# FFN phases two to four of a two-layer macaron trunk: a second pair of hidden chunks as seven block products, and the late pair one chunk later

## The chip, the cores and the metric

The kernel runs on one core of one Trainium2 chip. The metric is the device time of one execution in microseconds; the time of a kernel is the median of three runs. Beside it stands one profiled execution, whose trace gives every instruction's start and length on each engine: PE (TensorE matmuls), PEld (its weight loads), DVE (VectorE), ACT (ScalarE), POOL (GpSimd), SP (SyncE, which issues nearly all DMAs).

## The reference

Two layers, each with three residual steps on x of 256 tokens by 1024, all in float32:

```python
def _swiglu(h, w_in, w_out):
    gate, up = jnp.split(h @ w_in, 2, axis=-1)
    return (jax.nn.silu(gate) * up) @ w_out
...
    for l in range(DEPTH):
        h = _swiglu(_rmsnorm(x, g[0]), ffn_w_in[l, 0], ffn_w_out[l, 0])
        x = x + 0.5 * _rmsnorm(h, g[1])
        h = _mixer(_rmsnorm(x, g[2]), ...)
        x = x + _rmsnorm(h, g[3])
        h = _swiglu(_rmsnorm(x, g[4]), ffn_w_in[l, 1], ffn_w_out[l, 1])
        x = x + 0.5 * _rmsnorm(h, g[5])
```

The hidden width of an FFN is 2816, so w_in is 1024 x 5632 and w_out 2816 x 1024. The mixer (attention and an mLSTM) is not touched by the change.

## The kernel before

**Phases.** The six residual steps are phases 0 to 5, run one after the other: FFN (0), mixer (1), FFN (2), FFN (3), mixer (4), FFN (5). "FFN phases two to four" are phases 2, 3 and 5. In the profile they begin at about 292, 473 and 762 us. The tokens are two tiles of 128.

**Float32 on TensorE.** Every operand is split in two parts, a high part in a reduced float32 form and the low rest; a product is three matmuls, high x high, low x high and high x low (mm3, lines 504 to 508). Weights come in pieces of 1 MB, DMA'd by SP into wr (every fourth piece into wx) and cut in two halves; halved (L291) makes wh of each on ACT (L295) and wl on DVE (L296).

**An FFN.** The hidden width is 11 chunks of 256. The steps that a chunk c goes through are named in a list, STEPS (L37):

- I c: load two pieces, and 48 matmuls of 512 columns for both token tiles; ACT and DVE make Silu(gate) x up (ffn_hidden, L637); planes (L645) reorders the words on ACT, SP turns them with a DMA transpose (L647), and ready joins them: hT (L653), then hh on ACT (L669) and hl on DVE (L670).
- L c: load and cut the chunk's output piece. O c: 24 matmuls of 512 columns into four banks bk, 12 for each token tile.
- S: one step of pair_tokens, which makes differences of the token blocks for the pair.
- P c: chunks c and c + 1 together (pair). Their two token tiles by two chunks by two halves of the inner width are 2 x 2 block matrices, computed by seven block products (product, L755) in place of eight; the four weight pieces are added to each other on DVE (pair_blocks, L322), each combination is cut like a weight, and the products are combined on DVE and ACT (L769 to L792) to h for token tile 0 and v for token tile 1, each with both chunks. Both are turned like a chunk's h; pair_ready joins them.
- The last chunk, 10, is not computed tokens by hidden units but turned (in_turned, L730 and L735), so that its result needs no transpose; ffn_turned combines it in su (L688 to L690). Its step I10 ends the list. Behind it the output parts of END, chunks 8, 9 and 10, stand written by hand: token 0 of 8, 9 and 10, then token 1.

**What sets the order.** The lines are recorded in program order, and a scheduler places each engine's instructions by its own priorities, so PE's stream mixes neighbouring steps; parts under high_priority (the pair's combinations, ffn_turned) are placed early. From "ending" to "running" (the output parts of END and the next phase's first matmuls) PE's order is the written one. Each engine runs its own list strictly in order. SP's queue holds weight loads and transposes together. Pools of wl, wh and a lent third one let the cutting run some ten halves ahead of PE. The weights lie in host memory in the order in which the steps load them; _pack takes it from STEPS.

In STEPS the pair is P7, behind O4 and ahead of L6 and O5; chunk 9 follows as I9, and the pair's joining is recorded in I9, behind the cut of its first piece (lines 871 and 872).

Of the kernel before, what the change touches and what calls it, by code (L numbers as in the profile page):

```python
# [33 lines left out]
CH = P  # L34
EPS = 1e-6
BIG = -1.0e30
STEPS = "I2 L1 S0 O0 I3 L2 S1 O1 I4 L3 S2 O2 I5 L4 O3 I6 L5 O4 P7 L6 O5 L7 O6 I9 L8 O7 I10 L9".split()  # L37
END = (8, 9, 10)
AHEAD = 2
AT = (0, 2, 6, 6, 9, 22, 24, 24, 26, 26, 36, 40, 30, 46, 34, 50, 46, 52, 52, 57, 61, 60, 61, 67, 67, 69, 71, 78, 74, 74, 80, 84)  # L40
# [19 lines left out]
def _pack(inp):  # L60


    f32 = np.float32
    x = np.asarray(inp["x"])
    w_in, w_out = np.asarray(inp["ffn_w_in"]), np.asarray(inp["ffn_w_out"])
    m_in, m_out = np.asarray(inp["mix_w_in"]), np.asarray(inp["mix_w_out"])
    g = np.asarray(inp["norm_gains"])
    w = np.empty((L * PIECES_LAYER, P, 2048), f32)

    def ffn(at, l, f):  # L70
        n = w_in[l, f].reshape(2, 4, P, 2, NC_FF, 256).transpose(0, 3, 2, 1, 4, 5)
        a = n.transpose(4, 0, 2, 3, 1, 5).reshape(NC_FF, 2, P, 2048)
        b = w_out[l, f].reshape(NC_FF, 2, P, D).transpose(0, 2, 1, 3).reshape(NC_FF, P, 2048)
        order = [a[0, 0], a[0, 1], a[1, 0], a[1, 1], b[0]]
        for step in STEPS:
            c = int(step[1:])
            if step[0] == "P":
                order += [n[kh, g, :, :, c:c + 2].reshape(P, 2048) for kh, g in ((0, 0), (0, 1), (1, 1), (1, 0))]
            elif step[0] in "IL":
                order += [a[c, 0], a[c, 1]] if step[0] == "I" else [b[c]]  # L80
        for piece in order + [b[END[-1]]]:
            w[at] = piece
            at += 1

    for l in range(L):
        at = l * PIECES_LAYER
        ffn(at, l, 0)
        at += PIECES_FFN
        for n, lo in enumerate(MIX_GROUPS):
            a = m_in[l][:, lo:lo + 512].reshape(2, 4, P, 512).transpose(0, 2, 1, 3)  # L90
            w[at + 2 * n:at + 2 * n + 2] = a.reshape(2, P, 2048)
        at += 2 * len(MIX_GROUPS)
        w[at:at + 4] = m_out[l].reshape(4, 2, P, D).transpose(0, 2, 1, 3).reshape(4, P, 2048)
        ffn(at + 4, l, 1)
    for i in range(2):
        w[i] = w[i].reshape(P, 4, 512).transpose(1, 0, 2).reshape(P, 2048)

    arrays = {
        "x": x.reshape(NT, P, 2, 512).transpose(0, 2, 1, 3),
        "w": w,  # L100
        "gpost": g[:, 1::2].reshape(L * 3, D),
        "lam": np.asarray(inp["da_lambda"]).reshape(L, 256),
    }
    arrays = {k: np.ascontiguousarray(v) for k, v in arrays.items()}
    gpre = g[:, 0::2].reshape(L, 3, KT, P).transpose(3, 0, 1, 2).reshape(P, L * 3 * KT)
    arrays["c0"] = np.concatenate([np.eye(P, dtype=f32), gpre], 1)

    inv = (f32(10000.0) ** (-np.arange(0, 64, 2, dtype=f32) / f32(64))).astype(f32)
    ang = np.arange(S, dtype=f32)[:, None] * inv[None, :]
    cos, sin = np.cos(ang).astype(f32), np.sin(ang).astype(f32)  # L110
    rope = np.stack([np.concatenate([cos, cos], 1), np.concatenate([-sin, sin], 1)])
    s = np.arange(P)[:, None]
    j = np.arange(P)[None, :]
    mask = np.where((s // CH == j // CH) & (s <= j), 0.0, BIG).astype(f32)
    first = (np.arange(S) % CH == 0)
    scan = np.stack([np.where(first, 0.0, 1.0), np.where(first, BIG, 0.0)]).astype(f32)

    def everywhere(v):
        return np.broadcast_to(np.asarray(v).reshape(1, -1), (P, np.asarray(v).size))

    parts = {
        "wg": m_in[:, :, 3072:3080].reshape(L, KT, P, 8).transpose(2, 0, 1, 3),
        "rope": rope.reshape(2, NT, P, 64).transpose(2, 0, 1, 3),
        "convw": np.asarray(inp["ml_conv_w"]).reshape(L, 4, 4, P).transpose(3, 0, 2, 1),
        "convb": np.asarray(inp["ml_conv_b"]).reshape(L, 4, P).transpose(2, 0, 1),
        "gda": np.asarray(inp["da_subln_g"]).T,
        "gml": np.asarray(inp["ml_norm_g"]).T,
        "gateb": everywhere(inp["ml_gate_b"]),
    }
    arrays["c1"] = np.concatenate([parts[n].reshape(P, -1) for n, _ in C1], 1)  # L130
    arrays["mask"] = mask
    arrays["scan"] = np.ascontiguousarray(np.broadcast_to(scan.reshape(1, 512), (100, 512)))
    return arrays


class _Trunk:
# [569 lines left out]
    def ffn(self, pre, gi_post):  # L706
# [3 lines left out]
        def in_piece(t, kh, pin, w):  # L710
            xh, xl = xT[t][kh]
            for k in range(4):
                self.mm3(pin, xh[:, k, :], xl[:, k, :], *self.cols(w, k),
                         start=kh == 0 and k == 0, stop=kh == 1 and k == 3)

        def out_part(c, t, h, wo):
            for hf in range(2):
                for k in range(2):
                    self.mm3(po[t][hf], *h[t][k], *self.cols(wo, 2 * k + hf),
                             start=c == 0 and k == 0, stop=c == NC_FF - 1 and k == 1)  # L720
# [20 lines left out]
        def ready(c, others):  # L741
            if c in sent:
                hT = self.ffn_joined(sent.pop(c), others)
                hs[c] = self.ffn_split([hT[:, t] for t in range(NT)])

        def chunk(c, pins):
            h = self.t2("h", (P, NT, 256))
            i = [self.ffn_hidden(pins[t], r[t], h[:, t]) for t in range(NT)]
            send(c, h)
            ready(c - 1, i[:1])  # L750
# [45 lines left out]
        def pair_ready(others):  # L796
            c, turned = sent.pop("pair")
            hT = [self.ffn_joined(v, others) for v in turned]
            for j in range(2):
                hs[c + j] = self.ffn_split([h[:, j] for h in hT])  # L800

        hs, po, wo, sent = {}, [], {}, {}
        kept = bool(xT)
# [48 lines left out]
            ready(0, [i])  # L852
        both, swap = list(self.both), 0
        tokens = self.pair_tokens(both, kept)
        for at, step in enumerate(STEPS):
            kind, c = step[0], int(step[1:])
            if kind == "P":
                pair(c)
            elif kind == "S":
                sums = next(tokens)  # L860
            elif kind == "L":
                if wo.get(c) is None:
                    wo[c] = self.piece()
            elif kind == "I":
                if c == 3:
                    g = self.load_gpost(gi_post)
                    yield "middle"
                ws = [self.piece()]
                cut = self.cut
                ws.append(self.piece())  # L870
                if "pair" in sent:
                    pair_ready([cut])
                for later in STEPS[at + 1:]:
                    if later[0] != "L":
                        break
                    wo[int(later[1:])] = self.piece()
                if c == END[-1]:
                    ready(c - 1, [self.cut])
                    break
                pins = [self.bank_pin() if swap else self.bank_tr() for _ in range(NT)]  # L880
                swap = 1 - swap
                for kh in range(2):
                    for t in range(NT):
                        in_piece(t, kh, pins[t], ws[kh])
                chunk(c, pins)
            else:
                if not po:
                    po = [[self.bank_bk() for _ in range(2)] for _ in range(NT)]
                for t in range(NT):
                    out_part(c, t, hs[c], wo[c])  # L890
# [574 lines left out]
```

## Time and profile before

| | us |
|---|---|
| median of three runs | 953.43 (953.31 to 953.56) |
| profiled execution | 954.38 |
| its span in the trace | 952.6 |
| granted TensorE clock, mean | 0.999 |
| phases 0, 1, 2, 3, 4, 5 begin at about | 0, 183, 292, 473, 653, 762 |

The span is what the trace covers, from the first instruction to the last; the profiled execution's own time is 1.8 us longer. Busy shares are means over the span. The page's sliced rows, 40 slices of 23.8 us each, show how even the load of the engines is (tenths; 9 is 90% or more):

```profile
DVE  7965885789767865795796578857897687558853
ACT  8966767577756866586587657666778478567662
```

The engine beside TensorE that is busiest is DVE; its 8s and 9s lie where the weight cutting of a phase's opening or of a pair falls.

### The profile page before, as it was taken

To read this page: it belongs to the slowest core of one execution; us is meant where nothing else is said; L and a number is where in the kernel's file an instruction comes from. 1 tells how busy PE (TensorE), PEld (TensorE's weight loads), DVE (VectorE), ACT (ScalarE), POOL (GpSimd) and SP (SyncE) were. 2 spreads that over 40 slices of the span, in tenths; PEclk is the share of its full clock that TensorE was granted. 3 is DMA by queue.
4 is the path that set the end of the run, shared out by engine and by line. 5 is a ranking of instruction groups with operands and counts; after the bars stand their busy time and mean duration, and the time that the engine had idled before them with its cause. 6 is when DMAs were issued, how large, how long until landed. Compare 5 with 4: busy or idle time off the path is not lost.

```text
span 952.6 us, 12113 instructions
## 1 busy us (share of the span) xinstructions
PE 944.1 (99%) x4475; PEld 779.7 (82%) x4475; DVE 705.4 (74%) x1011; ACT 648.9 (68%) x1013; POOL 28.0 (3%) x57
## 2 busy tenths in 40 slices
PE   9999999999999999999999999999999999999997
PEld 6888888888788888888888888888888888888885
DVE  7965885789767865795796578857897687558853
ACT  8966767577756866586587657666778478567662
POOL 2000000000010000000000000000000100000000
PEclk9999999999999999999999999999999999999999
DMA  9985476346362885467558663753554449654731
GB/s 342 343 300 151 150 273 201 133 137 235 109 250 89 313 243 182 155 238 234 181 201 284 184 224 128 277 161 133 180 197 157 153 160 291 233 175 143 284 83 45
DMA packets 69881, 189.33 MB, mean 199 GB/s; under 512 B 45274, under 2 KB 46426, under 8 KB 49086
## 3 DMA queue, kind: packets, MB, share of 16 engines
q1 hardware_dynamic: 69246, 187.95, 58.5%
q8 instruction: 35, 0.57, 0.2%
q10 hardware_dynamic: 576, 0.61, 0.2%
q14 instruction: 24, 0.20, 0.1%
HBM read 177.01 MB, written 1.05 MB: 187 GB/s over the span
## 4 chain that ended last, share of the span: by engine, by line
PE 94%; ACT 2%; DMA 1%; DVE 1%; issue 1%; SPq 0%; POOLq 0%; DVEq 0%; ACTq 0%
PE pin L506 11%; PE pin L508 11%; PE pin L507 11%; PE bk L508 10%; PE bk L506 10%; PE bk L507 10%; PE ptr L506 5%; PE ptr L508 5%; PE ptr L507 5%; PE ptr L755 4%; PE pin L755 3%; PE pin L730 2%; PE ptr L730 1%; PE ptr L532 1%; PE ptr L1087 1%; PE pin L735 1%
## 5 line engine op out<-in xcount | busy, mean ns | idle before, releaser
L296 DVE TENSOR_TENSOR wl<-wr,wh 128x1024 fp32r<-128x1024 f32 x262 | 314.7, 1222 | 96.7 <-ACT wh L295 90.7
L295 ACT ACTIVATE wh<-wr 128x1024 fp32r<-128x1024 f32 x262 | 270.1, 1053 | 67.3 <-PE pin L508 18.7
L506 PE MATMUL pin<-wh,both 128*128 128x512 f32 x496 | 196.5, 397 | 0.1
L508 PE MATMUL pin<-wh,both 128*128 128x512 f32 x496 | 193.4, 390 | 0.0
L507 PE MATMUL pin<-wl,both 128*128 128x512 f32 x496 | 193.3, 390 | 0.0
L507 PE MATMUL bk<-wl,hh 128*128 128x512 f32 x352 | 137.1, 389 | 0.0
L506 PE MATMUL bk<-wh,hh 128*128 128x512 f32 x352 | 136.6, 390 | 0.0
L508 PE MATMUL bk<-wh,hl 128*128 128x512 f32 x352 | 135.2, 390 | 0.1
L506 PEld LDWEIGHTS pin<-wh,both 128*128 128x128 f32 x496 | 93.3, 188 | 19.7 <-issue 0.7
L508 PEld LDWEIGHTS pin<-wh,both 128*128 128x128 f32 x496 | 93.1, 188 | 19.9
L507 PEld LDWEIGHTS pin<-wl,both 128*128 128x128 f32 x496 | 93.3, 188 | 18.0
L296 DVE TENSOR_TENSOR wl<-wx,wh 128x1024 fp32r<-128x1024 f32 x62 | 75.3, 1222 | 30.4 <-ACT wh L295 30.4
L295 ACT ACTIVATE wh<-wx 128x1024 fp32r<-128x1024 f32 x62 | 64.5, 1052 | 22.2 <-PE ptr L508 6.8
L508 PEld LDWEIGHTS bk<-wh,hl 128*128 128x128 f32 x352 | 66.1, 188 | 14.4 <-DVE hl L670 0.5
L507 PEld LDWEIGHTS bk<-wl,hh 128*128 128x128 f32 x352 | 66.1, 188 | 13.5
L506 PEld LDWEIGHTS bk<-wh,hh 128*128 128x128 f32 x352 | 66.1, 188 | 13.3
L507 PE MATMUL ptr<-wl,both 128*128 128x512 f32 x192 | 74.7, 389 | 0.0
L508 PE MATMUL ptr<-wh,both 128*128 128x512 f32 x192 | 74.7, 389 | 0.0
L506 PE MATMUL ptr<-wh,both 128*128 128x512 f32 x192 | 73.4, 389 | 0.0
L653 ACT ACTIVATE hT<-h 128x1024 uint16<-128x1024 uint16 x36 | 49.0, 1360 | 15.3 <-DMA h<-planes 15.2
L645 ACT ACTIVATE planes<-h 128x1024 uint16<-128x1024 uint16 x36 | 37.9, 1052 | 19.4 <-DVE h L637 19.2
L670 DVE TENSOR_TENSOR hl<-hT,hh 128x256 fp32r<-128x256 f32 x80 | 30.3, 420 | 19.3 <-ACT hh L669 19.3
(263 smaller groups left out, 1288.7 us busy)
## 6 DMA issues: line engine op xcount, KB each, us to landing
wr<-in_w_dram SPq DMA_DIRECT2D x131, 1024.0 KB, 5.1
wx<-in_w_dram SPq DMA_DIRECT2D x31, 1024.0 KB, 4.9
gpost<-in_gpost_dram SPq DMA_DIRECT2D x6, 512.0 KB, 6.2
wr<-in_w_dram SPq DMA_DIRECT2D x2, 512.0 KB, 7.2
wr<-in_w_dram SPq DMA_DIRECT2D x3, 256.0 KB, 5.5
x<-in_x_dram SPq DMA_DIRECT2D x3, 256.0 KB, 5.9
h<-planes SPq DMA_TRANSPOSE x36, 4.4
out_dram<-x SPq DMA_DIRECT2D x2, 256.0 KB, 2.1
```

Source lines behind the costliest of these rows:

```text
L295: ia = nc.scalar.activation(hi, raw, AF.Copy)
L296: iv = nc.vector.tensor_tensor(lo, raw, hi.bitcast(F32), op=ALU.subtract)
L506: mm(ps, xh, wh, start=start, stop=False)
L507: mm(ps, xh, wl, start=False, stop=False)
L508: mm(ps, xl, wh, start=False, stop=stop)
L532: nc.tensor.transpose(ptr[:, k, :], x[:, (4 * hf + k) * P:(4 * hf + k + 1) * P], self.ident)
L645: nc.scalar.activation(planes, h.bitcast(U16).rearrange("p (n u) -> p u n", u=2), AF.Copy)
L653: i = self.nc.scalar.activation(hT.rearrange("p a b n -> p (a b n)").bitcast(U16).rearrange("p (n u) -> p u n", u=2), turned.rearrange("p ...
L670: return ia, self.nc.vector.tensor_tensor(hl, h, hh.bitcast(F32), op=ALU.subtract)
L730: self.nc.tensor.matmul(b, self.cols(w[kh], k)[0][:, c], both[kh][:, k].rearrange("p i t -> p (i t)"), start=kh == 0 and k == 0, stop=Fals ...
L735: self.nc.tensor.matmul(b[:, 0:NT * P], self.cols(w[kh], k)[1][:, c], both[kh][:, k, 0:NT].rearrange("p i t -> p (i t)"), start=False, sto ...
L755: self.nc.tensor.matmul(b, st[:, k, :], self.cols(w, k)[mv], start=new and k == n == 0, stop=k == 3 and n == 2, skip_group_check=True)
```

## The change

The list of steps becomes two. ONE is the old list and serves phase 0 alone (the phase that makes its own token blocks, kept False). TWO serves phases 2, 3 and 5: chunks 4 and 5 become a pair P4 directly behind O1 and S2; chunk 7 is a chunk of its own again; the late pair is P8, chunks 8 and 9; chunk 10 follows at once. The pair's joining is not recorded ahead of the next input step's weights if that step is I10, but behind the cut of chunk 9's output piece.

```diff
-STEPS = "I2 L1 S0 O0 I3 L2 S1 O1 I4 L3 S2 O2 I5 L4 O3 I6 L5 O4 P7 L6 O5 L7 O6 I9 L8 O7 I10 L9".split()
+ONE = "I2 L1 S0 O0 I3 L2 S1 O1 I4 L3 S2 O2 I5 L4 O3 I6 L5 O4 P7 L6 O5 L7 O6 I9 L8 O7 I10 L9".split()
+TWO = "I2 L1 S0 O0 I3 L2 S1 O1 S2 P4 L3 O2 L4 O3 I6 L5 O4 I7 L6 O5 P8 L7 O6 L8 O7 I10 L9".split()
 END = (8, 9, 10)
...
-        for step in STEPS:
+        for step in TWO if l or f else ONE:
...
-        for at, step in enumerate(STEPS):
+        steps = TWO if kept else ONE
+        for at, step in enumerate(steps):
...
                 ws = [self.piece()]
                 cut = self.cut
                 ws.append(self.piece())
-                if "pair" in sent:
+                if "pair" in sent and c != END[-1]:
                     pair_ready([cut])
-                for later in STEPS[at + 1:]:
+                for later in steps[at + 1:]:
                     if later[0] != "L":
                         break
                     wo[int(later[1:])] = self.piece()
                 if c == END[-1]:
+                    if "pair" in sent:
+                        pair_ready([self.cut])
                     ready(c - 1, [self.cut])
                     break
```

One line is added near the top, so most of the changed kernel's line numbers are one higher: L756 is the product, L646 planes, L648 the transpose, L654 hT, L670 and L671 hh and hl, L731 and L736 in_turned, L689 the copies to su, L323 the adds. The rows below are the order of an engine's instructions; the digits behind a name tell buffers apart.

On PE in phase 2, before, behind the pair: the last matmuls of the earlier output parts (bk), and then chunk 9's own products into pin.

```order
L508 MATMUL bk_3200<-wh_3926,hl_3856 128x512
L506 MATMUL bk_3200<-wh_3930,hh_3855 128x512
L507 MATMUL bk_3200<-wl_3929,hh_3855 128x512
L508 MATMUL bk_3200<-wh_3930,hl_3856 128x512
L506 MATMUL pin_4041<-wh_3994,both_2824 128x512
L507 MATMUL pin_4041<-wl_3993,both_2824 128x512
```

In the changed kernel, at the same place: the pair's last product (ptr_3952), five matmuls of O7, and chunk 10's turned products.

```order
L756 MATMUL ptr_3952<-wh_3936,both_3192 128x512
L508 MATMUL bk_3200<-wl_4070,hh_4000 128x512
L509 MATMUL bk_3200<-wh_4071,hl_4001 128x512
L507 MATMUL bk_3200<-wh_4075,hh_4000 128x512
L508 MATMUL bk_3200<-wl_4074,hh_4000 128x512
L509 MATMUL bk_3200<-wh_4075,hl_4001 128x512
L731 MATMUL pin_4191<-both_2824,wh_4139 128x512 x2
```

Further on, the turned products end and O8's token 0 begins, whose operand hh_4170 is the pair's.

```order
L736 MATMUL ptr_4194<-both_2833,wl_4148 128x256 x2
L736 MATMUL ptr_4194<-both_2833,wl_4152 128x256 x2
L507 MATMUL bk_3197<-wh_4105,hh_4170 128x512
L508 MATMUL bk_3197<-wl_4104,hh_4170 128x512
L509 MATMUL bk_3197<-wh_4105,hl_4171 128x512
```

Chunk 9's 48 matmuls are gone from between the pair and the first use of its words. In phases 3 and 5, 20 matmuls of O7 stand where phase 2 has five.

On ACT in phase 2, before, behind the pair: the pair's Silu, the planes of h and v, and the joinings hT.

```order
L267 ACTIVATE u_3810<-u_3810,rs_589_2968 128x512
L645 ACTIVATE planes_3902<-h_3812 128x1024
L295 ACTIVATE wh_4128<-wr_4125 128x1024
L295 ACTIVATE wh_4132<-wr_4125 128x1024
L645 ACTIVATE planes_3920<-v_3811 128x1024
L653 ACTIVATE hT_4011<-h_3812 128x2x512
L669 ACTIVATE hh_4015<-hT_4011 128x256
```

In the changed kernel the same stretch holds chunk 10's copies to su and its Silu too; hh_4170 is O8's operand for token 0, hh_4178 that of O9.

```order
L689 ACTIVATE su_4265<-pin_4191 128x256
L689 ACTIVATE su_4265<-pin_4192 128x256
L646 ACTIVATE planes_4065<-v_3956 128x1024
L268 ACTIVATE su_4265<-su_4265 128x256
L654 ACTIVATE hT_4166<-h_3956 128x2x512
L670 ACTIVATE hh_4170<-hT_4166 128x256
L689 ACTIVATE su_4278<-ptr_4193 128x256
L689 ACTIVATE su_4278<-ptr_4194 128x256
L654 ACTIVATE hT_4168<-v_3956 128x2x512
L268 ACTIVATE su_4278<-su_4278 128x256
L670 ACTIVATE hh_4172<-hT_4168 128x256
L670 ACTIVATE hh_4178<-hT_4166 128x256
```

Two copies that read in_turned's first banks have moved ahead of the planes of v. In phase 3 of the changed kernel the copies stand behind the joinings:

```order
L646 ACTIVATE planes_5610<-v_5501 128x1024
L654 ACTIVATE hT_5711<-h_5502 128x2x512
L670 ACTIVATE hh_5715<-hT_5711 128x256
L654 ACTIVATE hT_5713<-v_5501 128x2x512
L670 ACTIVATE hh_5717<-hT_5713 128x256
L670 ACTIVATE hh_5723<-hT_5711 128x256
L670 ACTIVATE hh_5725<-hT_5713 128x256
L689 ACTIVATE su_5810<-pin_5736 128x256
```

Both orders are the scheduler's; phase 5 has the one of phase 3.

On DVE in phase 2, before, around the step S2 (the difference aT and its split both): splits of weights and the results of chunks 2 and 3.

```order
L357 TENSOR_TENSOR aT_638_3193<-qk,wt 128x512
L296 TENSOR_TENSOR wl_3239<-wr_3237,wh_3240 128x1024
L670 TENSOR_TENSOR both_3192<-aT_638_3193,both_3192 128x4x128
L296 TENSOR_TENSOR wl_3229<-wr_3227,wh_3230 128x1024
L296 TENSOR_TENSOR wl_3233<-wr_3227,wh_3234 128x1024
L637 SCALAR_TENSOR_TENSOR h_3047<-pin_3046,rs_589_2968,sil_3075 128x256
L296 TENSOR_TENSOR wl_3243<-wr_3237,wh_3244 128x1024
L637 SCALAR_TENSOR_TENSOR h_3171<-ptr_3121,rs_566_2883,sil_3172 128x256
L296 TENSOR_TENSOR wl_3249<-wr_3247,wh_3250 128x1024
L637 SCALAR_TENSOR_TENSOR h_3171<-ptr_3122,rs_589_2968,sil_3175 128x256
```

In the changed kernel:

```order
L358 TENSOR_TENSOR aT_638_3193<-qk,wt 128x512
L297 TENSOR_TENSOR wl_3239<-wr_3237,wh_3240 128x1024
L671 TENSOR_TENSOR both_3192<-aT_638_3193,both_3192 128x4x128
L297 TENSOR_TENSOR wl_3229<-wr_3227,wh_3230 128x1024
L297 TENSOR_TENSOR wl_3233<-wr_3227,wh_3234 128x1024
L638 SCALAR_TENSOR_TENSOR h_3047<-pin_3046,rs_589_2968,sil_3075 128x256
L297 TENSOR_TENSOR wl_3243<-wr_3237,wh_3244 128x1024
L638 SCALAR_TENSOR_TENSOR h_3171<-ptr_3121,rs_566_2883,sil_3172 128x256
L297 TENSOR_TENSOR wl_3249<-wr_3247,wh_3250 128x1024
L323 TENSOR_TENSOR qk<-wx_3360,wr_3362 128x1024
L638 SCALAR_TENSOR_TENSOR h_3171<-ptr_3122,rs_589_2968,sil_3175 128x256
L323 TENSOR_TENSOR wt<-wx_3360,wr_3362 128x1024
```

S2 has kept its place; the first adds of P4's weight blocks (qk and wt are the halves of the sum) follow it where splits of chunk 4's weights stood.

## The prediction

> **What bounds the kernel now.** The page's busy shares come first, then the shares of the chain that ended last.
>
> ```profile
> span 952.6 us, 12113 instructions
> PE 944.1 (99%) x4475; PEld 779.7 (82%) x4475; DVE 705.4 (74%) x1011; ACT 648.9 (68%) x1013; POOL 28.0 (3%) x57
> ...
> PE 94%; ACT 2%; DMA 1%; DVE 1%; issue 1%; SPq 0%; POOLq 0%; DVEq 0%; ACTq 0%
> ```
>
> The end is set by TensorE from the first microsecond to the last: 99% busy, and 94% of the chain. The waits of PE, next, as engine and line, what was waited for, total us, times, longest:
>
> ```profile
> PE bk L495 <- PEq L1455: 0.8, 1, 0.8
> PE ptr L454 <- DMA x<-in_x_dram: 0.7, 1, 0.7
> PE bk L482 <- ACT wh L472: 0.2, 1, 0.2
> ```
>
> All three lie at the start; none lies in a phase that the change touches. So the time is the number of matmuls times their pitch, as long as operands are there. The chain (start, length, what) gives the pitch:
>
> ```profile
> 160.39 1.81 PE pin L730 x8
> 163.11 0.95 PE pin L735 x8
> ...
> 401.96 2.72 PE pin L755 x12
> ...
> 424.63 2.72 PE ptr L755 x12
> ```
>
> Twelve 512-column matmuls take 2.72 us: 0.2267 us each. The 256-column ones of L735 take 0.95 / 8 = 0.119 us.
>
> **What goes.** A pair as block products is 7 x 12 = 84 matmuls where two chunks of their own have 2 x 48 = 96. FFN phases two to four are phases two, three and five of the six, counted from zero; each gets one pair more, P4, and the late pair moves from chunks 7, 8 to 8, 9. That is 12 matmuls fewer in each of three phases: 36 x 0.2267 = **8.16 us** less on PE. The matmul group says that one "lasts" 389 ns, which would make 14.0 us; but that is a latency under pipelining, and the pitch is what adds up.
>
> ```profile
> L755 PE MATMUL ptr<-wh,both 128*128 128x512 f32 x128 | 41.7, 389 | 0.0
> ```
>
> The Trainium skill, page "TensorE: Matmul & The Clock Gate", section "Back-to-back issue gap", gives a sustained spacing of about 131 ns for 512 columns in a stream of weight loads and matmuls, and N/2.4 + 2.5 ns = 216 ns for one alone. The first would make the gain an estimated 4.7 us, the second 7.8; the trace's 0.2267 us stands in such a stream and contradicts the first.
>
> **What is added beside PE.** The groups (total us, mean ns, idle ahead):
>
> ```profile
> L296 DVE TENSOR_TENSOR wl<-wr,wh 128x1024 fp32r<-128x1024 f32 x262 | 314.7, 1222 | 96.7 <-ACT wh L295 90.7 <-PE bk L507 3.6 <-PE bk L508 1.7
> L295 ACT ACTIVATE wh<-wr 128x1024 fp32r<-128x1024 f32 x262 | 270.1, 1053 | 67.3 <-PE pin L508 18.7 <-PE ptr L755 9.8 <-PE bk L508 9.0
> L322 DVE TENSOR_TENSOR wr<-wr,wr 128x1024 f32<-128x1024 f32 x6 | 7.1, 1221 | 4.7 <-DMA wr<-in_w_dram 4.7
> L784 DVE TENSOR_TENSOR h<-ptr,u 128x512 f32<-128x512 f32 x4 | 2.7, 686 | 1.7 <-PE ptr L755 1.7
> L792 DVE SCALAR_TENSOR_TENSOR v<-v,rs,u 128x512 f32<-128x512 f32 x4 | 3.0, 750 | 0.0
> L637 DVE SCALAR_TENSOR_TENSOR h<-pin,rs,sil 128x256 f32<-128x256 f32 x38 | 18.1, 480 | 2.3 <-ACT sil L267 2.3
> L267 ACT ACTIVATE u<-u,rs 128x512 f32<-128x512 f32 x4 | 2.9, 726 | 5.0 <-DVE u L790 5.0
> ```
>
> One more pair brings DVE 8 adds of 1.22 us, 6 more weight splits of 1.22 (14 halves in place of 8), 7 combining operations (five like L784, two like L792: 4.9 us) and takes 4 of L637's away (1.9 us): 9.8 + 7.3 + 4.9 - 1.9 = **20.1 us of DVE a phase**, 60 in all, so 705 becomes about 766 of some 948 (81%). ACT gets 6 casts of 1.05 and a few small ones, about 7 us a phase. DMA bytes and the number of transposes stay.
>
> Spread over a phase this fits; inside a pair it does not. A pair wants (8 + 14) x 1.22 + 4.9 = 31.7 us of DVE against 84 x 0.2267 = 19.0 of PE, 12.7 too much, so it lives on splits made ahead. The windows of the old pair (bounds, length, then busy time of PE, PEld, DVE, ACT, POOL, clock, DMA share, GB/s) show whether that is enough; first phase two's opening up to chunk 3, where P4 will stand, then the stretch ahead of the old pair, then that pair in phases two and three:
>
> ```profile
> 292.00:346.00 54.00, 54.00 (x245) 44.82 (x243) 43.62 (x57) 39.75 (x58) 1.62 (x3) 1.00 0.70 222
> 346.00:402.00 56.00, 56.00 (x248) 46.36 (x248) 35.84 (x39) 33.30 (x40) 0.00 (x0) 1.00 0.59 200
> 402.00:427.40 25.40, 25.40 (x113) 21.02 (x112) 22.55 (x25) 20.67 (x26) 0.00 (x0) 1.00 0.61 212
> ...
> 582.00:609.20 27.20, 27.20 (x122) 22.52 (x121) 24.80 (x26) 19.43 (x23) 0.00 (x0) 1.00 0.61 232
> ```
>
> PE never waited, and DVE was idle 25.40 - 22.55 = 2.85 and 27.20 - 24.80 = 2.40 us within the pair: that is the margin. P8 keeps such a stretch ahead of it. P4 does not: in the opening, 54 us, DVE idles 54.00 - 43.62 = 10.4 us, against 20.2 in the 56 ahead of the old pair. (The third token step, S2, costs nothing new: its three operations stand at the same rows of DVE's order before and after.) The splits made ahead must hold 12.7 us of DVE work for P4, and 10.4 are free. **Bounds for waits inside the pairs: nothing (the old pair's rows) to 12.7 - 10.4 = 2.3 us a phase, 6.9 in all. I take 1 in all**, near the old pair's rows, since those are the same instructions and the matmuls of O2, O3 and O6, O7 stand among the products as cover.
>
> **The join, where I choose a loss.** The old pair's result was wanted only after chunk 9's own 48 matmuls. Phase three's chain shows how long the way is:
>
> ```profile
> 607.73 1.37 PE ptr L755 x6
> ...
> 613.82 0.73 ACT u L267
> 614.54 1.00 ACT planes L645
> ...
> 615.56 7.01 DMA h<-planes
> ...
> 622.65 0.04 ACT hT L653
> ...
> 626.09 0.43 DVE hl L670
> ...
> 626.57 0.50 PE bk L508
> ```
>
> The last product ends at 609.1 (call it E); the first tile's turned words land at 622.57, E + 13.5, and PE waited about 0.5 us at 626.1 for the low part (a wait that the change removes: **-0.5**). ACT's timeline in phase two (start, length; E = 427.35) shows both tiles:
>
> ```profile
> 430.50 1.06 ACT L645 ACTIVATE planes<-h 128x1024 uint16<-128x1024 uint16 x1
> ...
> 433.44 1.06 ACT L645 ACTIVATE planes<-v 128x1024 uint16<-128x1024 uint16 x1
> 434.76 1.38 ACT L653 ACTIVATE hT<-h 128x1024 uint16<-128x1024 uint16 x1 [0.27 <-DMA h<-planes]
> ...
> 442.87 1.37 ACT L653 ACTIVATE hT<-v 128x1024 uint16<-128x1024 uint16 x1 [2.31 <-DMA v<-planes]
> ```
>
> From the end of planes, the first tile took 3.2 us there (434.76 - 431.56), the second 8.4 (442.87 - 434.50); in phase three the first took 7.0. I take the mean of these, 6.2, with 3.2 and 8.4 as ends, and for the second tile 6.6 from the same rows and the queue's landing times:
>
> ```profile
> DMA to landing us min/median/max: 5.3/6.0/7.0
> ```
>
> In the changed order nothing but the rest of O7 and chunk 10's turned products (in_turned) stands between E and O8. in_turned has 32 matmuls of 512 columns and 32 of 256: 7.25 + 3.81 = 11.06 us, with two small transposes of rows 11.3. Each token-0 output part is 12 matmuls, 2.72 us.
>
> Phase two: 5 matmuls of O7 are left, so O8 starts at E + 1.1 + 11.3 = E + 12.4 and O9 at 15.1. ACT ends the first planes near E + 5.1 (four casts are queued ahead; 4.2 in the old row), the words land near 11.3, hT and hh (1.37 and about 0.4) follow: operands at 12.7 to 13.1, a stall of 0.3 to 0.7. But the operand for O9's token 0 is queued on ACT behind the second tile's hT, and the second planes stand behind two copies of chunk 10's first group, which wait for PE at about E + 6.7. They end near 8.6, land near 15.2, and hT, a Silu and two hh put O9's operand at 17.6: 2.1 us after PE, which is at 15.5 by then. **Phase two loses 2.4**, between 0 (landing after 3.2) and 4.2 (after 8.4).
>
> Phase three: 20 of O7 are left (4.5 us), so O8 is at E + 15.8, O9 at 18.5, O10 at 21.2. Both hT stand on ACT ahead of chunk 10's copies. Landing near 14.6 gives O9's operand at 17.2, in time; but the copies, adds and Silu of chunk 10 then start late and end at 21.5 to 22.3: **0.6**, between 0 and 2.5. Phase five has the same order and no loads of a next phase on SP: **0**.
>
> **Sum**, against the profiled execution's own 954.38 us (span 952.6 and 1.8 outside): -8.16 - 0.5 + 2.4 + 0.6 + 1 = -4.7, so 949.7. The three runs' median, 953.43, is 0.95 lower than the profiled one; taken from there, **948.8**.
>
> **Rivals.**
> *Full gain* (no wait anywhere): 953.43 - 8.66 = 944.8. For it: PE idles nowhere but for 0.5 us. Against it: the landing after 8.4 us in phase two.
>
> *The join becomes the bound; slower.* If the two transposes run one behind the other at 7.0 us each, the first tile lands at E + 12.1 and the second at 19.1. In phase two O9's operand is then at 21.5, 6.4 us late; in phases three and five O9's at 21.3 (2.8 late) and chunk 10's chain another 2.5. That is 6.4 + 5.3 + 5.3 = 17.0: 953.43 - 8.66 + 1 + 17.0 = 962.8. It decides once the three joins cost more than 8.66 - 1 + 1.9 = 9.6 us together, a landing at about E + 17 in all three. The rows are against it: in phase two the second tile's planes were cut while the first was landing, and no landing took more than 8.4.
>
> *VectorE becomes the bound in the early pair; no change.* If the 2.3 us of the bound appear in each phase, 6.9 us of waits take most of the gain: 953.43 - 8.66 + 3.0 + 6.9 = 954.7. It decides from 3.7 us in all, where the sum passes 951.5. The deficit of 12.7 us and the busier opening speak for it, the 2.4 us of DVE left idle inside the old pair against it.
>
> *The tensor clock falls.* The windows grant 1.00 throughout and the longest idle stretch is about 0.5 us, so no row shows what a longer one does; the start-up matmuls, which ran from a standstill, are slower than the 389 ns above:
>
> ```profile
> L495 PE MATMUL bk<-const-bfloat16-1.0 128*128 128x512 bf16 x8 | 3.7, 596 | 0.8 <-PEq L1455 0.8
> ```
>
> If phase two's join reaches its upper bound of 4.2 us, and the matmuls behind it run at 389 / 596 = 0.65 of their pace for as much work, that is 1.8 more of a wait and 4.2 / 0.65 - 4.2 = 2.3 of slow matmuls: 948.8 + 4.1 = 952.9. The Trainium skill, page "TensorE: Matmul & The Clock Gate", section "What's actually happening", has the clock halved after an idle window of about 3.4 us; no run here shows it.
>
> *It does not do what it says:* the scheduler undoes it, 953.4. The order has the 36 matmuls gone, so hardly any chance.
>
> **How the numbers follow.** Forecast with partial waits (946.5 to 951.5) 0.50; full gain (943.5 to 946.5) 0.17; VectorE 0.13; join slower 0.13; clock 0.05; nothing 0.02. About 0.2%, 1.9 us, can be told from no change here: below 951.5 is faster (0.67), 951.5 to 955.3 the same (0.20: VectorE, clock, nothing), above it slower (0.13). The range leaves out most of the slower case and the edge of the full gain: 944.5 to 955.5.
>
> **What would show it.** Right: 36 fewer matmuls at the old pitch; PE's gaps only ahead of O9's first matmul (hh or hl of the late pair) in phase two, 2 us, and ahead of O10's in phase three; DVE near 766 us; P4 and P8 with full PE. Wrong: PE waits for wl or wh inside P4; a gap over 3 us ahead of O8 or O9; a granted clock below 1.00 behind a gap; landings beyond E + 17.

## The result, and the profile after

The changed kernel takes **948.88 us** (six runs, 947.47 to 949.17) beside 953.84 us of the kernel before (six runs, 953.31 to 954.52): a ratio of 0.9945, 95% interval 0.9932 to 0.9958. Its profiled execution took 949.07 us, 5.3 less than the one before. The forecast was 948.8.

The page, in the lines that were shown of before:

```profile
span 947.3 us, 12104 instructions
PE 936.2 (99%) x4439; PEld 772.3 (82%) x4439; DVE 757.5 (80%) x1062; ACT 664.5 (70%) x1028; POOL 28.3 (3%) x57
...
PE 97%; DMA 1%; ACT 1%; DVE 0%; issue 0%; SPq 0%; POOLq 0%; DVEq 0%; ACTq 0%
```

36 matmuls fewer (4475 to 4439), and TensorE is still the bound. DVE is busy for 52 us more and is at 80%. (60 were forecast, and the durations of its instructions do add up to 60.6 us more; but neighbours overlap a little, so that two splits in a row take 2.35 us and not 2.44.) The waits of PE are no longer all at the start; beside three such there are now:

```profile
PE bk L507 <- ACT hh L670: 1.7, 1, 1.7
...
PE ptr L507 <- DVE h L785: 0.9, 3, 0.6
```

One wait of an output part (bk) for hh, and three short ones of an input part's bank (ptr) for the pair's combination h (L785). The chain of phase two's end (start, length, what) shows the first; the late pair's last product ends at 445.37:

```profile
442.65 2.72 PE ptr L756 x12
...
452.32 0.39 ACT su L689
452.71 0.94 ACT planes L646
...
453.68 6.67 DMA v<-planes
...
460.37 1.35 ACT hT L654
461.71 0.26 ACT su L268
461.97 0.62 ACT hh L670 x2
...
462.64 0.50 PE bk L507
```

Read from the bottom: O9's first matmul waits for the second hh of tile 0, which stands on ACT behind hT of tile 1 (v), which waits 6.67 us for its transpose. The start of that matmul comes 1.83 us beyond the usual pitch. The second kind, from the same view at the end of P4 in phase two:

```profile
379.21 1.37 PE ptr L756 x6
...
380.61 1.07 ACT wh L296
...
381.70 0.04 DVE wl L297
381.74 1.11 issue
382.85 0.69 DVE h L785
...
383.68 0.47 PE ptr L507
```

The matmul at 383.68 is chunk 6's first. It writes a ptr bank, and the pair's last products lie in the ptr banks until DVE has read them; the read (L785) stands on DVE behind a weight split of 1.2 us. DVE's timeline shows that split:

```profile
381.70 1.23 DVE L297 TENSOR_TENSOR wl<-wr,wh 128x1024 fp32r<-128x1024 f32 x1 [1.72 <-ACT wh L296]
```

DVE stood idle for 1.72 us ahead of it, until ACT had made its wh. The product that L785 reads, the last but one of the seven, had been done since about 377.6, so the read waited for its turn in DVE's queue and not for data. Chunk 6's matmul starts 0.77 us late there, and 0.32 in phases three and five.

The starts of the phases, by the first matmul of each phase's prenorm transposes (L532, now L533) in the timeline, before and after:

| phase | before | after | difference |
|---|---|---|---|
| 2 | 473.37 - 291.19 = 182.18 | 473.72 - 291.34 = 182.38 | +0.20 |
| 3 | 653.51 - 473.37 = 180.14 | 650.91 - 473.72 = 177.19 | -2.95 |
| 5, to the last matmul's start | 945.85 - 761.51 = 184.34 | 940.56 - 758.53 = 182.03 | -2.31 |
| 0, 1 and 4 (unchanged) | 291.19 + 108.00 | 291.34 + 107.62 | -0.23 |

Phase two gained nothing at all; phases three and five gained about the 2.7 us (12 matmuls at their pitch) that each was to gain.

### The profile page after: what moved, and what is told of

It reads as the page before. It is cut to its first block, busy times and chain, and to the rows that moved or that the text cites. A ratio compares the mean times of both kernels' runs of the same rounds, so it can differ in the third digit from the quotient of the medians.

```text
span 947.3 us, 12104 instructions
## 1 busy us (share of the span) xinstructions
PE 936.2 (99%) x4439; PEld 772.3 (82%) x4439; DVE 757.5 (80%) x1062; ACT 664.5 (70%) x1028; POOL 28.3 (3%) x57
## 4 chain that ended last, share of the span: by engine, by line
PE 97%; DMA 1%; ACT 1%; DVE 0%; issue 0%; SPq 0%; POOLq 0%; DVEq 0%; ACTq 0%
PE pin L507 11%; PE pin L509 11%; PE pin L508 11%; PE bk L507 10%; PE bk L509 10%; PE bk L508 10%; PE ptr L756 8%; PE pin L756 6%; PE ptr L507 4%; PE ptr L509 3%; PE ptr L508 3%; PE pin L731 2%; PE ptr L731 1%; PE ptr L533 1%; PE ptr L1091 1%; PE pin L736 1%
## 5 line engine op out<-in xcount | busy, mean ns | idle before, releaser
L507 PE MATMUL pin<-wh,both 128*128 128x512 f32 x448 | 177.0, 398 | 0.0
L509 PE MATMUL pin<-wh,both 128*128 128x512 f32 x448 | 174.7, 390 | 0.0
L508 PE MATMUL pin<-wl,both 128*128 128x512 f32 x448 | 174.6, 390 | 0.0
L509 PE MATMUL bk<-wh,hl 128*128 128x512 f32 x352 | 133.1, 389 | 0.0
L509 PEld LDWEIGHTS pin<-wh,both 128*128 128x128 f32 x448 | 84.1, 188 | 18.0
L507 PEld LDWEIGHTS pin<-wh,both 128*128 128x128 f32 x448 | 84.3, 188 | 17.5 <-issue 0.7
L508 PEld LDWEIGHTS pin<-wl,both 128*128 128x128 f32 x448 | 84.2, 188 | 16.2
L297 DVE TENSOR_TENSOR wl<-wx,wh 128x1024 fp32r<-128x1024 f32 x62 | 75.4, 1222 | 10.4 <-ACT wh L296 10.4
L756 PE MATMUL ptr<-wh,both 128*128 128x512 f32 x224 | 73.3, 389 | 0.0
L507 PE MATMUL ptr<-wh,both 128*128 128x512 f32 x144 | 55.0, 391 | 0.9 <-DVE h L785 0.9
L508 PE MATMUL ptr<-wl,both 128*128 128x512 f32 x144 | 55.7, 389 | 0.0
L509 PE MATMUL ptr<-wh,both 128*128 128x512 f32 x144 | 55.7, 389 | 0.0
L756 PE MATMUL pin<-wh,both 128*128 128x512 f32 x168 | 55.1, 389 | 0.0
L654 ACT ACTIVATE hT<-h 128x1024 uint16<-128x1024 uint16 x33 | 45.0, 1364 | 6.2 <-DMA h<-planes 5.9
```

The costliest lines, as they stand in the source:

```text
L297: iv = nc.vector.tensor_tensor(lo, raw, hi.bitcast(F32), op=ALU.subtract)
L507: mm(ps, xh, wh, start=start, stop=False)
L508: mm(ps, xh, wl, start=False, stop=False)
L509: mm(ps, xl, wh, start=False, stop=stop)
L654: i = self.nc.scalar.activation(hT.rearrange("p a b n -> p (a b n)").bitcast(U16).rearrange("p (n u) -> p u n", u=2), turned.rearrange("p ...
L756: self.nc.tensor.matmul(b, st[:, k, :], self.cols(w, k)[mv], start=new and k == n == 0, stop=k == 3 and n == 2, skip_group_check=True)
```

## The experiments

All times below are medians, with the ratio to the kernel before, which ran beside them: 953.57 us in the first four, 953.92 in the last four. The diffs are against the changed kernel. Phases zero and one are the same program in all but the last kernel, and still phase two begins anywhere from 289.8 to 291.3 us in their traces. So beside the medians this table gives the touched phases alone, from one trace of each kernel but the one with a third pair (starts as in the table above, phase five to its last matmul's start):

| kernel | phase 2 | phase 3 | phase 5 | sum |
|---|---|---|---|---|
| before | 182.18 | 180.14 | 184.34 | 546.66 |
| changed | 182.38 | 177.19 | 182.03 | 541.60 |
| other bank | 181.23 | 176.73 | 181.60 | 539.55 |
| tile 0 first | 180.49 | 177.11 | 182.04 | 539.65 |
| late place alone | 183.89 | 179.67 | 184.36 | 547.92 |
| early pair, old late place | 181.11 | 177.71 | 182.82 | 541.64 |
| both edits | 179.74 | 176.66 | 181.62 | 538.02 |
| joining at its old place | 182.80 | 177.16 | 182.04 | 542.00 |
| both edits, new list everywhere | 179.37 | 179.59 | 181.62 | 540.58 |

**Which bank the chunk behind a pair takes.**

```diff
             if kind == "P":
                 pair(c)
+                swap = 1
```

> The changed kernel, but the chunk behind a pair takes its two banks from pin, not from ptr. Theory (the waits behind P4, start-to-start 0.8, 0.3 and 0.3 us beyond the pitch, are waits for the ptr banks that the pair's last combinations still read on VectorE): they go, about 1.4 us less than the changed kernel, 947.5. Rival (chunk 6 would wait for its weights or VectorE at that place anyway): TensorE waits for wh or wl there instead, 948.9.

947.69 us; ratio 0.9943 (0.9927 to 0.9959). The runs lie far apart (945.69 to 950.82), so the median can't tell 1.4 us; the trace can. (In the three runs at 949 to 951 the granted clock was 0.996 on average, in the three at 945.7 to 946.4 it was 0.998 or 0.999. So the clock seems to have fallen somewhere in the longer ones; no trace of them was kept.) The windows around P4 and chunk 6 in phases two, three and five (bounds, length, busy PE, PEld, DVE, ACT, POOL, clock, DMA share, GB/s):

```profile
350.00:386.00 36.00, 36.00 (x161) 29.80 (x160) 31.63 (x34) 27.34 (x32) 0.00 (x0) 1.00 0.59 214
528.00:566.00 38.00, 38.00 (x169) 31.45 (x169) 35.24 (x38) 29.29 (x33) 0.00 (x0) 1.00 0.61 219
814.00:853.00 39.00, 39.00 (x174) 32.30 (x173) 36.06 (x39) 29.32 (x34) 0.00 (x0) 1.00 0.64 223
```

PE is busy for all of each, so the three waits were for the bank, and nothing took their place. Phase two's wait for hh stays (1.2 and 0.4 us beyond the pitch there). The touched phases are 2.05 us shorter than in the changed kernel.

**Tile 0 first.** For each tile hT and both chunks' hh and hl are made before the next tile is touched.

```diff
-            hT = [self.ffn_joined(v, others) for v in turned]
+            ops = [[self.ffn_operand() for _ in range(2)] for _ in range(NT)]
+            for t in range(NT):
+                hT = self.ffn_joined(turned[t], others)
+                for j in range(2):
+                    self.ffn_hilo(hT[:, j], *ops[t][j])
             for j in range(2):
-                hs[c + j] = self.ffn_split([h[:, j] for h in hT])
+                hs[c + j] = [[tuple(v[:, k] for v in ops[t][j]) for k in range(2)] for t in range(NT)]
```

> The changed kernel, but the joining makes both chunks' operands of token tile 0 before it touches tile 1. Theory (phase two's 1.8 us ahead of O9 come from O9's tile-0 operand being queued on ScalarE behind the joining of tile 1, which waits for its transpose): the wait goes, 947.1, no wait in its place. Rival (the transposes land too late as such): the wait moves to the next output part that needs tile 1 or chunk 10, 948.9.

946.20 us; ratio 0.9925 (0.9913 to 0.9937). ACT's timeline at phase two's join:

```profile
454.94 1.38 ACT L654 ACTIVATE hT<-h 128x1024 uint16<-128x1024 uint16 x1 [2.19 <-DMA h<-planes]
456.35 0.72 ACT L670 ACTIVATE hh<-hT 128x256 fp32r<-128x256 f32 x2
459.44 1.36 ACT L654 ACTIVATE hT<-v 128x1024 uint16<-128x1024 uint16 x1 [1.82 <-DMA v<-planes]
```

Both hh of tile 0 now stand ahead of tile 1's hT. Tile 1 still lands late (459.4, no earlier in the phase than before), and nobody waits: of the 1.8 us, 0.2 ahead of O8 is left. So the order on ACT was the cause, not the landing of tile 1 as such. The touched phases are 1.95 us shorter than in the changed kernel.

**The late place alone.** The old list with P8 in place of P7, and no P4.

```diff
-TWO = "I2 L1 S0 O0 I3 L2 S1 O1 S2 P4 L3 O2 L4 O3 I6 L5 O4 I7 L6 O5 P8 L7 O6 L8 O7 I10 L9".split()
+TWO = "I2 L1 S0 O0 I3 L2 S1 O1 I4 L3 S2 O2 I5 L4 O3 I6 L5 O4 I7 L6 O5 P8 L7 O6 L8 O7 I10 L9".split()
```

> The list with the late pair at chunks 8, 9 and no early pair (chunks 4 and 5 as before the change): as many matmuls as before. Theory (the late place costs phase two's join of 1.8 us and saves phase three's old wait of 0.3): about 1.5 us over the kernel before. Rival (the join is late only because the second pair loads VectorE and ScalarE): the same time as before, less 0.3.

954.29 us (eleven runs); ratio 1.0006 (0.9998 to 1.0015), which is 0.2 us less to 1.4 more. The theory's 1.5 lies at one edge, the rival's -0.3 at the other, so the time alone does not tell them apart. The trace does: phase two is 1.7 us longer than before, phase three 0.5 shorter, the touched phases 1.3 longer, as the theory has it. The wait of PE is there too:

```profile
PE bk L507 <- ACT hh L670: 1.5, 1, 1.5
```

That wait is ahead of O8, not O9, in phase two: here tile 0's own words landed 6.3 us after its planes, and ACT had both hT ahead of O8's hh. A late join is there without any P4; VectorE's extra load is not needed for it.

**The early pair with the old late place.**

```diff
-TWO = "I2 L1 S0 O0 I3 L2 S1 O1 S2 P4 L3 O2 L4 O3 I6 L5 O4 I7 L6 O5 P8 L7 O6 L8 O7 I10 L9".split()
+TWO = "I2 L1 S0 O0 I3 L2 S1 O1 S2 P4 L3 O2 L4 O3 I6 L5 O4 P7 L6 O5 L7 O6 I9 L8 O7 I10 L9".split()
```

> The early pair at chunks 4, 5, and the other pair where it was, at 7, 8, with chunk 9 by itself: the same 36 matmuls fewer. Theory: no join at the end of a phase, the waits behind P4 stay: 948.9 - 1.8 + 0.3 = 947.4. Rival (two pairs closer together starve TensorE of splits in the second): waits for wl in P7, 949 or more.

947.61 us; ratio 0.9939 (0.9927 to 0.9951). That is the theory's sum, but not by its terms: the wait at the end of phase two is gone and the three for the bank stay, and there are three short ones ahead of O4 (0.58, 0.34 and 0.55 us beyond the pitch) that no theory had.

```profile
PE bk L507 <- ACT hh L670: 1.0, 3, 0.4
PE ptr L507 <- DVE h L785: 0.9, 3, 0.6
```

By the trace the touched phases take as long as in the changed kernel (541.64 and 541.60 us); phase two began 1.5 us earlier in this execution, so that the median met the theory is partly luck. No wait for wl or wh in P7, so the rival falls.

**Both edits together.**

> The changed kernel with both edits: pin banks behind a pair, and both operands of token tile 0 made before tile 1 is joined. Theory (two independent waits): their savings add, 948.9 - 1.4 - 1.8 = 945.7, and TensorE has no wait over 0.3 us in phases two, three and five. Rival (one wait hides the other): no better than the better of the two, 946.2 to 947.

944.33 us; ratio 0.9900 (0.9887 to 0.9914): both waits are gone, and the kernel beats the changed one by 4.6 us of the medians, more than the 3.2 of the two. One wait is left in the touched phases, the third row:

```profile
PE bk L496 <- PEq L1464: 0.8, 1, 0.8
PE ptr L455 <- DMA x<-in_x_dram: 0.4, 1, 0.4
PE bk L507 <- ACT hh L670: 0.3, 1, 0.3
```

Phase two takes 179.74 us there (290.86 to 470.60), 2.6 less than in the changed kernel, as the two waits of phase two (0.77 and 1.83) say. Of the 4.0 us between the two profiled executions (949.07 and 945.03), 0.5 lie in phases zero and one, which are the same program. The touched phases are 3.6 shorter, of which the waits make 3.0.

**The joining at its old place.**

```diff
-                if "pair" in sent and c != END[-1]:
+                if "pair" in sent:
                     pair_ready([cut])
...
-                    if "pair" in sent:
-                        pair_ready([self.cut])
                     ready(c - 1, [self.cut])
```

> The changed kernel, but the pair's joining is recorded where it was before, behind the cut of the next input step's first weight half. Every engine's instructions stand in the same order as in the changed kernel. Theory (the scheduler's order alone counts): 948.9, the same wait of 1.8 us in phase two. Rival (the later place spares ScalarE or SyncE something): 1 to 3 us slower.

948.14 us; ratio 0.9941 (0.9927 to 0.9954). That half of the change does nothing: the scheduler makes the same order of both. As a second execution of the same order it also shows how far the join's wait varies: 1.44 us ahead of O8 and 0.89 ahead of O9 here, 0.09 and 1.83 in the changed kernel's trace. From the end of its planes to its joining, tile 0 took 7.0 us here (449.18 to 456.17), and 5.6 there (450.45 to 456.06).

**A third pair.** Both edits, and chunks 6 and 7 as P6; the join of the pair before is recorded inside the next pair.

```diff
+TWO = "I2 L1 S0 O0 I3 L2 S1 O1 S2 P4 L3 O2 L4 O3 P6 L5 O4 L6 O5 P8 L7 O6 L8 O7 I10 L9".split()
...
             ready(c - 1, [i])
+            if "pair" in sent:
+                pair_ready([i])
```

> As the kernel with both edits, and chunks 6 and 7 a pair too: three pairs in a row in phases two, three and five, 36 matmuls fewer again, 60 us of VectorE more (87% busy). Theory that VectorE is covered by splits made ahead: 945.7 - 8.2 = 937.5. Theory that the cover is used up by then (each pair wants 12.7 us more of VectorE than TensorE takes, and only two output parts stand between the pairs): waits for wl inside P6 and P8 of 3 to 10 us a phase, 946 to 967.

987.07 us; ratio 1.0349 (1.0335 to 1.0364), worse than the bad end of the expectation. TensorE has 72 matmuls fewer than before the change, and waits:

```profile
PE bk L507 <- ACT hh L670: 24.0, 7, 6.4
PE bk L509 <- DVE hl L671: 4.7, 2, 2.3
PE ptr L756 <- DVE v L780: 3.7, 1, 3.7
PE pin L756 <- DVE wl L297: 1.3, 3, 0.4
```

The windows in phase two: P6 up to O4's first matmul at 404.2, the 6.4 us ahead of it in which PE stood, and the 10 us behind it; then a second gap ahead of 443.6, and the stretch behind that.

```profile
372.00:404.00 32.00, 24.80 (x107) 19.55 (x105) 31.44 (x31) 21.79 (x25) 0.00 (x0) 0.94 0.60 198
397.50:404.00 6.50, 0.33 (x2) 0.00 (x0) 6.50 (x7) 6.42 (x8) 0.00 (x0) 0.68 1.07 331
...
404.00:414.00 10.00, 7.71 (x18) 5.65 (x19) 9.54 (x13) 3.59 (x6) 0.00 (x0) 0.52 0.73 247
...
440.83:444.24 3.41, 1.07 (x5) 0.55 (x4) 3.41 (x6) 3.41 (x5) 0.00 (x0) 1.00 1.10 392
444.24:447.65 3.41, 3.41 (x10) 2.65 (x9) 3.41 (x4) 2.27 (x4) 0.00 (x0) 0.50 0.96 389
```

DVE is busy for 31.4 of the 32 us, and for all of the stretch in which PE stands: VectorE has no room left there, as the second theory said. But hardly any of the waiting is for wl: the pair's own combinations stand in the same queue as the splits and come late, so the words are turned late and O4 waits for hh. ACT is as full in that stretch (6.42 of 6.50 us), its queue mixes casts of weights with the pair's Silu, planes and joining in the same way, and the chain into O4's matmuls (386 to 408) runs mostly through it. Which of the two engines sets the time, and what recording the joining inside the next pair adds, was not told apart. And the tensor clock, 1.00 in the windows of the kernels above, is granted at 0.52 and 0.50 behind the gaps, so part of the loss is matmuls at a slower pitch.

**The new list in phase zero too.** Both edits, and TWO everywhere.

> As the kernel with both edits, and the new list in phase zero too, 12 matmuls fewer there. Theory that a phase's opening leaves VectorE enough room: 945.7 - 2.7 = 943.0. Rival (phase zero makes its own token blocks and token steps on VectorE, so the splits for P4 are late): TensorE waits for wl in phase zero's P4 for 1 to 5 us, 944 to 948.

944.84 us; ratio 0.9918 (0.9904 to 0.9931): no better than without. Phase zero is shorter by 3.7 us than in the trace with both edits alone (phase one starts at 179.44, against 183.10) and has no wait inside P4; phase one starts at 182.08 to 183.60 in all the other traces, so the gain is 2.6 to 4.2, and the theory's 2.7 fits. But phase three, whose text is the same, is 2.9 us longer (466.72 to 646.31, against 470.60 to 647.26): 2.0 us of it is a wait ahead of O8. Its chain:

```profile
619.74 2.28 DVE wl L297 x2
622.02 0.02 issue
622.03 0.33 SPq L289
622.36 0.05 issue
622.41 6.29 DMA h<-planes
...
628.79 0.79 ACT hT L654
...
630.02 0.35 ACT su L689
630.37 1.24 ACT hT L654
631.61 0.27 ACT hh L670
...
631.92 0.50 PE bk L507
```

SP held a weight load that waited for its buffer, until DVE had made the splits (622.02), and the transpose, whose planes had been ready since 621.5, stood behind it for 0.9 us. ACT's queue cost another 1.3 us: a copy of chunk 10 and tile 1's joining stand between tile 0's joining and O8's hh, which begins 2.7 us behind its hT here and 1.4 us behind in the kernel with both edits alone (625.72 to 627.13). So recording tile 0 first does not by itself fix the order; the scheduler placed tile 1 ahead again. That list in phase zero has changed what the scheduler does in phase three; why was not followed up.

## Why the prediction came out right, step by step

The total was right (948.8 against 948.88) partly by terms that cancel, and from a base, 953.43 us, that six runs put 0.4 higher. By the profiled executions:

| term | forecast | measured |
|---|---|---|
| 36 matmuls at the pitch | -8.16 | -8.16 (36 fewer, still twelve in 2.72 us) |
| phase three's old wait | -0.5 | -0.3 (the start beyond the pitch) |
| join, phase two | +2.4 | +1.9 |
| join, phase three | +0.6 | 0 |
| join, phase five | 0 | 0 |
| waits in the pairs | +1 | +1.4, by another mechanism |
| rest | 0 | -0.1 |
| sum | -4.7 | -5.3 |

- **The pitch, not the duration.** The 14.0 us that the durations would make and the 4.7 us by the Trainium skill's sustained spacing (page "TensorE: Matmul & The Clock Gate", section "Back-to-back issue gap") are both out: with the new waits removed the kernel is 9.6 us faster than before (944.33 against 953.92; 8.2 to 10.8 by the interval). 8.16 + 0.3 lies in that, the other two do not. In the traces the touched phases take 546.66 us before and 538.02 there, 8.6 less.
- **Phase three's old wait** was 0.27 us and not 0.5: the 0.5 was the distance from one matmul's start to the next, and 0.23 of that is the pitch.
- **Phase two's join** was the right place and the right reason: O9's operand for tile 0 queued on ACT behind tile 1's hT. The run with tile 0 first shows it by taking the wait away with no earlier landing. The landings were near the means taken (5.6 and 6.7 us after the planes, 6.2 and 6.6 taken).
- **Phase three's join** was put at 0.6 us by landings that were taken too late. The pair ended at 621.47, the second tile's words landed at 634.2, 12.7 us behind (14.6 taken), and the first hh of chunk 10 began at 640.43; O8 began at 637.22, 15.75 behind (15.8 forecast), so that O10 was due at 642.7. ACT's timeline there, and the window with PE full:

```profile
634.22 1.38 ACT L654 ACTIVATE hT<-v 128x1024 uint16<-128x1024 uint16 x1 [3.08 <-DMA v<-planes]
...
640.43 0.29 ACT L670 ACTIVATE hh<-su 128x128 fp32r<-128x128 f32 x1
```

```profile
622.00:642.00 20.00, 20.00 (x105) 17.11 (x104) 13.34 (x25) 12.43 (x22) 0.15 (x2) 1.00 0.64 187
```

- **Waits in the pairs** is the step that failed. It said that splits for P4 would be a little late. None was; the windows of the opening and of P4 in phase two:

```profile
292.00:346.00 54.00, 54.00 (x246) 44.82 (x245) 47.36 (x61) 38.60 (x57) 1.62 (x3) 1.00 0.68 219
...
353.00:381.80 28.80, 28.80 (x129) 23.85 (x128) 25.37 (x28) 20.90 (x25) 0.00 (x0) 1.00 0.58 219
```

The working set 31.7 us of DVE against the 19.0 of the products alone, and got its 12.7 us from that; the cover that it named it did not count. 43 matmuls of O2 and O3 stand among the products, so P4 lasts 28.8 us (127 matmuls at the pitch, 352.99 to 381.77), and the deficit is about 2.9 us. The opening took up 47.36 - 43.62 = 3.7 us of its 10.4 free ones; DVE was idle for 3.4 us even inside P4. The cost came at the pair's end instead, from the bank that the next chunk writes. Chunks of their own take ptr and pin in turn, from chunk 2 on: in the old list five of them (2 to 6) stand ahead of the pair and the one behind it takes pin, in the new list two (2 and 3), and the one behind takes ptr, which the pair's last products hold. The prediction looked for operands and not for banks, and its 1 us met the measured 1.4 by chance.
- **The rivals.** Full gain was the nearest: the kernel with both edits reaches its time (944.33 against 944.8), and the two new waits go by moving instructions. The join as the bound (962.8) fell; the words of the late pair did not queue up (with two pairs at most 7.3 us from the end of planes, in phase three of the kernel with the new list everywhere; 8.1 with three). Other transposes take longer where no matmul waits for them: chunk 0's in phase two 8.5 us before and up to 9.9 in these runs. VectorE as the bound did not occur with two pairs; with a third it is full, beside ScalarE. The clock did not fall behind the changed kernel's wait of 1.7 us in its trace, though the last section shows that such a wait is close to it.

## What to carry to other kernels

Where an engine's share is 99%, count instructions at their pitch; then look, for every step that is moved, not only at what its operands wait for but at which buffer its result is written to, and who still reads it. In a queue that runs in order, what is needed first must stand first: two casts put ahead of a joining that waits for a DMA were worth about 1.7 us here (waits of 1.9 down to 0.2). Room on an engine can be used up all at once: the second pair cost no wait for VectorE's splits, and with a third one, which has the joining of the pair before recorded inside it, the kernel took 43 us more than with two, with VectorE and ScalarE both full and the clock at half behind the gaps.

## What was not expected of the hardware

The tensor clock fell to half behind short gaps. In the third-pair kernel a gap of 2.3 us ahead of 443.6 was followed by matmuls 0.43 us apart from 444.5 to 447.5, and the windows above show the clock at 1.00 up to 444.24 and at 0.50 from there to 447.65; gaps of 3.7 to 6.4 us were followed by the same. Behind waits of 1.7 us (the changed kernel) and 2.0 us (the new list in phase zero too) the pitch stayed at 0.23.

The length of the gap is not all of it. In that trace every change of the granted clock lies a whole number of 3.413 us behind the first one, as on a fixed grid. The window from 440.83 to 444.24 is one cell of that grid, with TensorE idle for 2.34 of its 3.41 us; in the cell ahead of the first fall, 396.45 to 399.87, it was idle for 2.04. The changed kernel's wait fell across two cells of its own grid:

```profile
458.29:461.70 3.41, 2.68 (x12) 1.81 (x10) 1.38 (x5) 1.47 (x3) 0.00 (x0) 1.00 0.48 56
461.70:465.12 3.42, 2.48 (x11) 1.93 (x12) 1.84 (x6) 1.59 (x7) 0.00 (x0) 1.00 0.00 0
```

TensorE was idle for 0.73 and 0.94 us there. The wait of 2.0 us fell across two cells too (0.77 and 1.24 us idle). In the ten traces of this case the clock fell behind every full-speed cell with 1.90 us of idle time or more, and behind none with 1.87 or less. The grid starts at another point of each execution (3.9 to 6.4 us into the span), so a wait of 2 us may cost the clock in one run and not in the next. That is a likely reason for the runs with a mean clock of 0.996 above; it is not shown.

The Trainium skill, page "TensorE: Matmul & The Clock Gate", section "What's actually happening", has the clock halved after an idle window of about 3.4 us. The halving and the length agree with the trace; that the window be idle throughout does not, since 1.90 us of its 3.41 were enough here.
